# Gating v: the first column piece of six blocks from x times scale, 1/rms and shift row at the read-out

## The chip, the cores and the metric

The kernel runs on one core of a Trainium2 chip. The metric is the device time of one execution, in microseconds (us). Engines are named as in the profile: PE (TensorE, with its weight loads as PEld), DVE (VectorE), ACT (ScalarE), POOL (GpSimd) and SP, which here only issues transfers. SBUF is the on-chip memory, PSUM the banks that PE accumulates into.

## The reference, cut to what matters

A prompt of 1024 rows and a sample of 32 rows, each 1024 wide, go through two layers. The change touches only the start of the first one: the conditioned norm, and the half v of the gating product.

```python
mod = silu(c) @ w_ada[i] + b_ada[i]
sh1, sc1, gt1, sh2, sc2, gt2 = split(mod, 6)
h = rmsnorm(x, g_norm[i, 0]) * (1 + sc1) + sh1
z = gelu(h @ w_in)
u, v = split(z, 2)
v = rmsnorm(v, g_v)
```

Prompt and sample have a conditioning row each. After it come a spatial mix of v in chunks of 128 rows, an output product, and a squared-ReLU channel product. The second layer has a pooling mixer in place of the gating. All is float32; a product of two float32 matrices is made of three products of split operands, high·high, low·high and high·low, where the high part is the operand rounded to the type fp32r and the low part is the rest.

## The kernel before

x is kept transposed in SBUF: three tiles of columns, of 384, 384 and 256 + 32 rows of the input (`acc[t]`). A tile is cut in blocks of 128: 0 to 2, 3 to 5, 6 and 7, and the sample's 32 rows as block 8. Each block is loaded, its squares are summed on ACT (L565), it is turned by eight PE transposes into PSUM (L580) in two halves, and DVE (L586) and ACT (L588) copy these to `acc`.

The conditioning vectors are slices of 256 columns of `mod`: slices 0 to 3 give the shift, 4 to 7 the scale `coef` = (1 + sc1)·g, later ones the rest. Slices 0 to 7 are multiplied on PE (L477), turned on DVE and gathered by small PE products (L459). From slice 8 on they are multiply-adds on DVE (tiles `aa`), two loads of 512 KB for each slice.

The norm of a tile needs 1/rms of its rows as a row spread over partitions. `spread` (L715) takes mean square, square root, reciprocal and one Newton step (DVE and ACT), ACT makes diagonal matrices of the result (L730), PE multiplies them with ones (L732, tile `pb_h`), and ACT copies the product (L893). `apply` (L853) then makes, for each of the eight k blocks of 128 features, mt = x·coef·r on DVE, the high part hh = mt + shift on ACT (L875) and the low part hl on DVE.

v has 2048 columns, worked on in four column pieces p of 512. For each piece the weight comes in four loads q of 256 rows of K (512 KB, through three raw slots). ACT makes its high part wh (L422), DVE its low part wl. A block of a piece is 24 products of 512 columns (8 k blocks × hh·wh, hh·wl, hl·wh), then `v_end` takes it out of PSUM: gelu on ACT (L941), square with a sum on ACT (L942), store.

All loads are in one list, `stream`, in order, issued on SP's queue as soon as their slot is free; `stream_to(kind, key)` steps through it and does what belongs to each item. `issue` (L395) issues, `do_w` splits a weight, `do_ada_pe` and `do_ada` do slices. The order of instructions up to the end of the sixth block is written out by hand (`tc.manual_schedule()`, L991 to L1047): instructions are issued on each engine in the written order.

That order is: x 0 to 2, statistics of tile 0, slices 4 and 0, weight 0, h of tile 0, then products of blocks 0 to 2 with the weight rows of q = 0 (`early_mm`, L973), the same for tile 1 with blocks 3 and 4, and so on for q = 1 to 3, with slices 4 + q and q ahead of each. Blocks 0 to 2 accumulate in the three banks `ps_dn` ("pd"), blocks 3 and 4 in the two banks `ps_up` ("pu"). Then follow the transposes of blocks 6 to 8, block 5 as a whole in a bank of `ps_ms` ("pm", three slots, which transposes, gathers and spreading use too), and the end, `v_end` of blocks 0 to 5 in turn with the weights of column piece 1:

```python
        ps = ps_ms("pv0_5")
        v_mm(ps, 0, 5, range(KB))
        next(h2)
        early_end((0,))
        stream_to("w", ("v", 1, 1))
```

After it comes the loop over `v_order` (L1073 to L1085): piece 1 for blocks 0 to 5, pieces 0 and 1 for blocks 6 to 8, pieces 2 and 3 for all. There a planner, `weave`, puts steps of the load list and other work between the blocks, by an estimate of the time that PE and DVE have used (`time["pe"]`, `time["dve"]`). pv1_0 below means piece 1 of block 0. L79 is the helper that records every DVE arithmetic instruction, so DVE's work is told apart by tile names.

Of the kernel before, what the change touches and what calls it, by code (L numbers as in the profile page):

```python
# [34 lines left out]
def tile_stream_encoder_step(  # L35
# [144 lines left out]
    def load_vectors(i, part):  # L180
        at = sum(k for _, k in rows[i][: part.start])
        for ap, k in rows[i][part]:
            nc.scalar.dma_start(vec_rows[i][at : at + k, :P], ap)
            at += k
# [6 lines left out]
    def turn_conditions():  # L191
        raw = vec_rows[2]
        nc.vector.memset(csil32, 0.0)
        act(out=raw[0:16, P : 2 * P], in_=raw[0:16, :P], func=AF.Silu)

        act(out=raw[0:16, 2 * P : 2 * P + 1], in_=epsT[0:16, :], func=AF.Sqrt)
# [181 lines left out]
    state = {"issued": 0, "next": 0, "raw": 0, "used": 0, "folds": 0}  # L378
    deferred = []

    def in_raw(k):
# [5 lines left out]
    x_rows = [  # L387
        room("h", t, f"x_rows{t}")
        .rearrange("p k n -> p (k n)")[:, : ncol[t] // P * D]
        .rearrange("p (b k n) -> p b k n", k=KB, n=P)  # L390
        for t in range(NT)
    ]
    junk = room("l", NT - 1, "xsq")

    def issue():  # L395
        while state["issued"] < len(stream):
            k = state["issued"]
            kind, key, ap, shape = stream[k]
            if in_raw(k):
                if state["raw"] == RAW_SLOTS:  # L400
                    return
                state["raw"] += 1
                r = t_raw(f"raw{k}")
            elif kind == "x":
                r = x_rows[key // 3][:, key % 3] if key < 8 else junk[:, :, P : 2 * P]
# [12 lines left out]

    def do_w(key, r):
        wh = work.tile([P, 1024], F32R, tag="W", bufs=W_SLOTS, name="wh_" + "_".join(map(str, key)))  # L420
        wl = work.tile([P, 1024], F32R, tag="W", bufs=W_SLOTS, name="wl_" + "_".join(map(str, key)))
        act(out=wh, in_=r, func=AF.Copy)  # L422
# [140 lines left out]
    def x_squares(b, r):  # L563
        nr = P if b < 8 else DEC
        act(  # L565
            out=junk[:nr, :, :P],
            in_=r[:nr],
            func=AF.Square,
            accum_out=ssx[:nr, b : b + 1],
        )  # L570

    def x_turn(b, r):
# [3 lines left out]
        for half in range(2):  # L576
# [8 lines left out]
            if half == 0 or t == 0:  # L585
                nc.vector.tensor_copy(dst, src)  # L586
            else:
                act(out=dst, in_=src, func=AF.Copy)  # L588


    x_turns = deque()

    def do_x(b, r):
        x_squares(b, r)
        if b < 3:
            x_turn(b, r)
        else:
            x_turns.append(lambda: x_turn(b, r))
# [10 lines left out]
    def stream_step():  # L609
# [18 lines left out]
        if in_raw(k):  # L628
            state["raw"] -= 1
# [84 lines left out]

    def spread(t, ss, tag, out, dg):  # L715
# [5 lines left out]
        ts(ms[:, :nb], ss[:, :nb], 1.0 / D, EPS, op0=ALU.mult, op1=ALU.add)  # L721
        act(out=r0[:, :nb], in_=ms[:, :nb], func=AF.Sqrt)
        nc.vector.reciprocal(out=r0[:, :nb], in_=r0[:, :nb])
        tt(out=q[:, :nb], in0=r0[:, :nb], in1=r0[:, :nb], op=ALU.mult)
        stt(out=q[:, :nb], in0=q[:, :nb], scalar=-0.5, in1=ms[:, :nb], op0=ALU.mult, op1=ALU.mult)
        stt(out=r0[:, :nb], in0=q[:, :nb], scalar=1.5, in1=r0[:, :nb], op0=ALU.add, op1=ALU.mult)
        yield False
        pb = ps_ms(f"pb_{tag}")
        for b, (c0, w) in enumerate(blk):
            act(out=dg[:w, c0 : c0 + w], in_=ident[:w, :w], func=AF.Copy, scale=r0[:w, b : b + 1])  # L730
        for b, (c0, w) in enumerate(blk):
            mm(pb[:, c0 : c0 + w], ones[:w, :], dg[:w, c0 : c0 + w], start=True, stop=True)  # L732
        out.append(pb)
# [119 lines left out]
    def apply(t, l, cf, sh, r, keep=False):  # L853
        hh[t] = room("h", t, f"hh{l}_{cf}_{t}", F32R)
        hl[t] = room("l", t, f"hl{l}_{cf}_{t}", F32R)
# [40 lines left out]

    def products(ps, n, terms):
# [8 lines left out]

    ssqv = small.tile([P, 9, 4], F32, name="ssqv")
# [25 lines left out]
    def v_end(ps, p, b):  # L933
# [3 lines left out]
        if b == 8:  # L937
# [21 lines left out]
    h0, h1, h2 = (first_norm(t) for t in range(NT))  # L959

    def early_mm(bs, q):

        wh, wl = witem[("v", 0, q)]
        for second in (False, True):
            for b in bs:
                t, c0 = b // 3, b % 3 * P
                tick(0.46 if second else 0.92)
                for k in range(2):
                    kb = 2 * q + k
                    a_h, a_l = hh[t][:, kb, c0 : c0 + P], hl[t][:, kb, c0 : c0 + P]  # L970
                    w = slice(k * 512, k * 512 + 512)
                    for a in (a_h,) if second else (a_h, a_l):
                        mm(  # L973
                            early_ps[b],
                            a,
                            (wl if second else wh)[:, w],
                            start=kb == 0 and a is a_h and not second,
                            stop=kb == KB - 1 and second,
                        )
# [5 lines left out]
    def conditions(q):  # L985

        stream_to("ada", (0, 4 + q, 1))
        stream_to("ada", (0, q, 1))
        pe_folds.pop(0)()

    with tc.manual_schedule():  # L991
        load_vectors(2, slice(0, 2))
        issue()
        load_vectors(2, slice(2, 4))
        load_vectors(0, slice(0, 1))
        load_vectors(1, slice(0, 1))
        turn_conditions()
        stream_to("x", 1)
        turn_vectors()
        stream_to("x", 2)  # L1000
        next(h0)
        conditions(0)
        statistics(h0)
        stream_to("w", ("v", 0, 0))
        pe_folds.pop(0)()
        for q in range(4):
            next(h0)
            if q == 0:
                late_lo.pop()()
            early_mm((0, 1, 2), q)  # L1010
            if q == 0:
                stream_to("x", 5)
                next(h1)
                x_turns.popleft()()
                x_turns.popleft()()
                next(h1)
                x_turns.popleft()()
                statistics(h1)
            next(h1)
            if q < 3:  # L1020
                conditions(q + 1)
                stream_to("w", ("v", 0, q + 1))
                early_mm((3,), q)
                pe_folds.pop(0)()
                early_mm((4,), q)
                if q == 2:
                    stream_to("x", 6)
            else:
                early_mm((3, 4), q)
        stream_to("x", 8)  # L1030
        while x_turns:
            x_turns.popleft()()
        next(h2)
        ps = ps_ms("pv0_5")
        v_mm(ps, 0, 5, range(KB))
        next(h2)
        early_end((0,))
        stream_to("w", ("v", 1, 1))
        early_end((1, 2))
        stream_to("w", ("v", 1, 2))  # L1040
        early_end((3,))
        stream_to("w", ("v", 1, 3))
        early_end((4,))
        statistics(h2)
        v_end(ps, 0, 5)
# [13 lines left out]
    rv = small.tile([P, 9], F32, name="rv")  # L1059
    rms = small.tile([P, 9, 2], F32, name="rms")  # L1060

# [11 lines left out]
    v_order = [(1, b) for b in range(6)] + [(p, b) for p in range(2) for b in range(6, 9)]  # L1073
# [600 lines left out]
```

## Time and profile before

| | us |
|---|---|
| three runs | 2173.76, 2173.64, 2171.72 |
| their median | 2173.64 |
| the profiled execution, its own time | 2173.74 |
| its span, first to last instruction | 2171.7 |
| mean granted clock of TensorE | 0.996 |

The profile is of one execution. Its page gives each engine's busy time and groups of instructions with their mean duration. The timeline lists instructions by engine: start, duration, engine, line, operation, output from inputs, shapes, count, and in brackets how long the engine stood idle before and what released it. Runs of like instructions that follow one another stand as one row with a count, and the duration is that of the whole row. A matmul's row lasts until its result is out, while the next one starts earlier, so a stretch of products is priced by the distance of their starts. Of the first 80 us, the table by line has these groups of the stage:

| group, first 80 us | count | busy us | mean ns |
|---|---|---|---|
| v products hh·wh, hl·wh, hh·wl (L973) | 40, 40, 40 | 18.8, 18.2, 11.8 | 471, 456, 414 |
| transposes of x (L580) | 64 | 10.8 | 331 |
| slices on PE (L477) | 128 | 9.1 | 427 |
| h: mt, hh, hl of 384 columns | 16 each | 9.1, 9.1, 9.2 | 613, 615, 616 |
| squares of x, 1024 columns (L565) | 8 | 8.4 | 1051 |

### The profile page before, as it was taken

What the parts mean: (1) busy time and instruction counts of PE and PEld (TensorE: products, weight loads), DVE (VectorE), ACT (ScalarE), POOL (GpSimd) and SP (SyncE); (2) the same over time, 40 slices, a digit from 0 to 9 for tenths busy, and PEclk for the clock granted to TensorE, in tenths of its full rate; (3) what the DMA queues carried; (4) which work ended last, traced back from release to release, by engine and by line L of the source; (5) the groups of instructions that cost most, each with busy time, mean ns of one, the idle gap of its engine ahead of it and who ended that gap; (6) DMA issues with size and microseconds to landing.
All of it is one profiled execution on the core that took longest, in us unless ns stands there. A gap on an engine that the chain in (4) does not pass through costs nothing.

```text
span 2171.7 us, 33210 instructions
## 1 busy us (share of the span) xinstructions
PE 2145.5 (99%) x13214; PEld 2078.1 (96%) x13214; DVE 1431.8 (66%) x2499; ACT 971.3 (45%) x1643; POOL 13.3 (1%) x30
## 2 busy tenths in 40 slices
PE   7999999999999999999999999999999999999998
PEld 5778899999999999999999999999999999999997
DVE  5688647566879548496747879869675554523377
ACT  4633422234447552323445566666555542313354
POOL 0000000000000000000000000000000000000001
PEclk9999999999999999999999999999999999999999
DMA  8386534343437454243645466565455552302255
GB/s 300 119 269 193 173 93 139 90 148 109 147 96 233 132 155 143 87 140 110 196 129 161 141 189 182 171 191 158 141 161 158 157 155 68 98 20 78 69 139 125
DMA packets 383262, 312.95 MB, mean 144 GB/s; under 512 B 39458, under 2 KB 346346, under 8 KB 383108
## 3 DMA queue, kind: packets, MB, share of 16 engines
q1 hardware_dynamic: 380452, 308.64, 46.8%
q8 instruction: 103, 1.69, 0.3%
q10 hardware_dynamic: 2144, 1.41, 0.2%
q0 software_dynamic: 512, 0.79, 0.1%
q14 instruction: 51, 0.42, 0.1%
HBM read 278.95 MB, written 31.84 MB: 143 GB/s over the span
## 4 chain that ended last, share of the span: by engine, by line
PE 93%; DVE 3%; DMA 2%; ACT 1%; issue 1%; ACTq 0%; DVEq 0%; SPq 0%
PE pg L902 11%; PE pg L903 11%; PE pg L904 11%; PE pf L902 11%; PE pf L904 11%; PE pf L903 11%; PE po L902 3%; PE po L903 3%; PE po L904 3%; PE pu L902 3%; PE pu L904 3%; PE pu L903 3%; PE pv L929 2%; PE pv L930 2%; PE pv L931 2%; PE pp L1532 1%
## 5 line engine op out<-in xcount | busy, mean ns | idle before, releaser
L902 PE MATMUL pg<-fh,wh_dn 128*128 128x384 f32 (+1 forms) x1536 | 495.8, 323 | 0.0
L902 PE MATMUL pf<-hh,wh_up 128*128 128x384 f32 (+1 forms) x1536 | 494.4, 322 | 0.0
L903 PE MATMUL pf<-hl,wh_up 128*128 128x384 f32 (+1 forms) x1536 | 493.1, 321 | 0.0
L904 PE MATMUL pf<-hh,wl_up 128*128 128x384 f32 (+1 forms) x1536 | 492.9, 321 | 0.2 <-DVE wl_up L79 0.2
L903 PE MATMUL pg<-fl,wh_dn 128*128 128x384 f32 (+1 forms) x1536 | 492.6, 321 | 0.4 <-DVE fl L79 0.4
L904 PE MATMUL pg<-fh,wl_dn 128*128 128x384 f32 (+1 forms) x1536 | 492.5, 321 | 0.0
L79 DVE TENSOR_TENSOR wl_up<-raw,wh_up 128x1024 fp32r<-128x1024 f32 x152 | 185.9, 1224 | 165.4 <-ACT wh_up L422 165.4
L902 PEld LDWEIGHTS pg<-fh,wh_dn 128*128 128x128 f32 x1536 | 288.3, 188 | 1.5 <-ACT fh L1121 0.6
L903 PEld LDWEIGHTS pg<-fl,wh_dn 128*128 128x128 f32 x1536 | 288.3, 188 | 1.5 <-DVE fl L79 0.7
L904 PEld LDWEIGHTS pf<-hh,wl_up 128*128 128x128 f32 x1536 | 288.6, 188 | 0.5 <-DVE wl_up L79 0.5
L903 PEld LDWEIGHTS pf<-hl,wh_up 128*128 128x128 f32 x1536 | 288.3, 188 | 0.4
L902 PEld LDWEIGHTS pf<-hh,wh_up 128*128 128x128 f32 x1536 | 288.2, 188 | 0.4
L904 PEld LDWEIGHTS pg<-fh,wl_dn 128*128 128x128 f32 x1536 | 288.3, 188 | 0.0
L422 ACT ACTIVATE wh_up<-raw 128x1024 fp32r<-128x1024 f32 x152 | 161.2, 1060 | 279.9 <-PE pf L903 213.6
L79 DVE TENSOR_TENSOR acc<-acc,pg 128x384 f32<-128x384 f32 (+1 forms) x336 | 174.2, 519 | 146.3 <-PE pg L904 145.7
L422 ACT ACTIVATE wh_dn<-raw 128x1024 fp32r<-128x1024 f32 x152 | 160.8, 1059 | 202.9 <-PE pg L903 170.6
L79 DVE TENSOR_TENSOR wl_dn<-raw,wh_dn 128x1024 fp32r<-128x1024 f32 x152 | 186.0, 1224 | 82.4 <-ACT wh_dn L422 82.2
L79 DVE SCALAR_TENSOR_TENSOR aa<-raw,csil,aa 128x512 f32<-128x512 f32 (+1 forms) x364 | 203.5, 623 | 8.0 <-DMA raw<-in_w_ada_dram 7.9
L1295 ACT ACTIVATE r<-pf 128x384 f32<-128x384 f32 (+1 forms) x192 | 86.6, 451 | 201.9 <-PE pf L904 199.2
L79 DVE TENSOR_TENSOR fl<-r,fh 128x384 fp32r<-128x384 f32 (+1 forms) x192 | 100.3, 523 | 85.4 <-ACT fh L1121 84.3
L902 PE MATMUL pu<-hh,wh_u 128*128 128x384 f32 (+1 forms) x384 | 125.8, 328 | 0.0
L902 PE MATMUL po<-ush,wh_o 128*128 128x384 f32 (+1 forms) x384 | 123.5, 322 | 0.0
(263 smaller groups left out, 2927.2 us busy)
## 6 DMA issues: line engine op xcount, KB each, us to landing
raw<-in_ffn_w_up_dram SPq DMA_DIRECT2D x152, 512.0 KB, 3.9
raw<-in_ffn_w_down_dram SPq DMA_DIRECT2D x152, 512.0 KB, 3.5
raw<-in_w_ada_dram SPq DMA_DIRECT2D x96, 512.0 KB, 4.3
raw<-in_sgu_w_in_dram SPq DMA_DIRECT2D x40, 512.0 KB, 4.4
xd<-acc SPq DMA_DIRECT2D x8, 1536.0 KB, 7.8
raw<-in_sgu_w_out_dram SPq DMA_DIRECT2D x24, 512.0 KB, 4.0
xo_r<-xd SPq DMA_DIRECT2D x32, 384.0 KB, 3.4
vd<-vt SPq DMA_DIRECT2D x32, 256.0 KB, 4.5
```

Source lines behind the costliest of these rows:

```text
L79: return op(out, *args, **kw)
L422: act(out=wh, in_=r, func=AF.Copy)
L902: mm(ps[:, :n], wh, rh, start=i == 0, stop=False)
L903: mm(ps[:, :n], wh, rl, start=False, stop=False)
L904: mm(ps[:, :n], wl, rh, start=False, stop=i == last)
L929: mm(ps[:m, :], a_h, wh[:, o : o + 512], start=k == 0, stop=False)
L930: mm(ps[:m, :], a_h, wl[:, o : o + 512], start=False, stop=False)
L931: mm(ps[:m, :], a_l, wh[:, o : o + 512], start=False, stop=k == KB - 1)
L1295: act(out=r[:, :n], in_=ps[:, :n], func=AF.Relu)
L1532: mm(ps[:, :n], wg[:, k, e * P : (e + 1) * P], A(t, 2 * g + k), start=k == 0, stop=k == 1)
```

## The change

For blocks 0 to 5 the first column piece of v (p = 0) is no longer multiplied from h but from x·scale: h·W = (x·coef·W)·r + shift·W, where r is 1/rms of the row, a scalar for each partition at the read-out. In parts:

- `scaled` makes the operands from `acc`: hx = x·coef on ACT, lx = x·coef − hx on DVE, in the rooms that hh and hl take later. Neither r nor the shift slices are needed for it.
- `shift_products` multiplies the shift, split in two columns, with the 8 k blocks of wh and wl: 16 products of 512 columns into `prow`, one row copied by ACT. `spread_shift` multiplies it with ones (one float32 product of 512 columns, `pbias`) and ACT copies it to an SBUF tile, `bias`.
- In `v_end`, for p = 0 and blocks 0 to 5, one DVE multiply-add makes ps·r + bias ahead of gelu, which now reads SBUF.
- `roots` makes r from the sums of squares (Abs_reciprocal_sqrt and a Newton step in place of square root, reciprocal and Newton step), per partition into `rv`.
- h itself is still needed for the other pieces. `full` spreads r as before and runs `apply` into the same tiles: for tile 0 between the products of blocks 3 to 5, for tile 1 between the products of pv1_0 and pv1_1.
- Blocks 3, 4 and 5 go together now; block 5 accumulates in its `ps_ms` slot from the start of that group. The transposes of blocks 6 to 8 follow the bias product, and the spreading of tile 1's r, pv1_0, and the spreading of tile 2's r follow them on PE.
- The load list is: x0, slice 4, weight 0, x1, x2, slice 5, weight 1, slice 6, weight 2, x3 to x5, slice 7, weight 3, slices 0 to 3, x6 to x8, then as before. At most eight early loads (slices and x5) are in flight. Low parts of piece 0's weights are made at written places (`late_lo`).
- g_norm, b_ada, pool_scale and g_v are loaded over POOL's queue instead of ACT's, and x2 over SP's instead of ACT's.

The instructions after pv1_2 stand in the same order on each engine as before.

```diff
-    for b in range(3):
-        add_x(b)
     for q in range(4):
-        for j in (8 + 2 * q, 9 + 2 * q, 2 * q, 2 * q + 1):
+        if q == 0:
+            add_x(0)
+        for j in (8 + 2 * q, 9 + 2 * q):
             add_ada(0, j)
         add_w(*v_item(0, q))
-        if q == 0:
-            for b in range(3, 6):
-                add_x(b)
+        for b in ((1, 2), (), (3, 4, 5), ())[q]:
+            add_x(b)
+    for j in range(8):
+        add_ada(0, j)
...
+            if k < first_ada and (kind == "ada" or key == 5):
+                if state["early"] == W_SLOTS // 2:
+                    return
+                state["early"] += 1
...
-                i = (nc.scalar if key == 2 else nc.sync).dma_start(
+                i = nc.sync.dma_start(
...
-        if key == ("v", 0, 0):
-            late_lo.append(lambda: tt(out=wl, in0=r, in1=wh.bitcast(F32), op=ALU.subtract))
+        if key[:2] == ("v", 0):
+
+            def low():
+                tt(out=wl, in0=r, in1=wh.bitcast(F32), op=ALU.subtract)
+                state["raw"] -= 1
+                issue()
+
+            late_lo.append(low)
...
+    def scaled(t, ks, c0, w):
...
+        for k in ks:
+            act(
+                out=hh[t][:, k, c0 : c0 + w],
+                in_=A(t, k, c0, w),
+                func=AF.Copy,
+                scale=coef[:, 0, 0, 0, k : k + 1],
+            )
+        for k in ks:
+            stt(
+                out=hl[t][:, k, c0 : c0 + w],
+                in0=A(t, k, c0, w),
+                scalar=coef[:, 0, 0, 0, k : k + 1],
+                in1=hh[t][:, k, c0 : c0 + w].bitcast(F32),
+                op0=ALU.mult,
+                op1=ALU.subtract,
+            )
+
+    def full(t):
+        cp = t_c(f"r_h0_{t}")
+        pb = diagonals(t, rv[:, 3 * t : 3 * t + 3], [(c * P, P) for c in range(3)], cp, f"h0_{t}")
+        act(out=cp[:, : ncol[t]], in_=pb[:, : ncol[t]], func=AF.Copy)
+        yield False
+        yield from apply(t, 0, 0, 0, cp, keep=True)
...
-        if b == 8:
+        if p == 0 and b < 6:
+            stt(out=vt, in0=ps, scalar=rv[:, b : b + 1], in1=bias[0], op0=ALU.mult, op1=ALU.add)
+            z = vt
+        elif b == 8:
...
+    def shift_products():
...
+        prow = ps_ms("prow")
+        for k in range(KB):
+            for w in witem[("v", 0, k // 2)]:
+                mm(
+                    prow[0:2, :],
+                    parts_of_shift[:, k, :],
+                    w[:, k % 2 * 512 : k % 2 * 512 + 512],
...
+    def spread_shift(row):
+        pbias = ps_ms("pbias")
+        mm(pbias, ones[0:2, :], row[0:2, :], start=True, stop=True)
+        bias.append(work.tile([P, 512], F32, tag="aa", bufs=2, name="shift_rows"))
+        act(out=bias[0], in_=pbias, func=AF.Copy)
...
+    front, rear = (0, 1, 2), (3, 4, 5)
...
+        scaled(0, (6, 7), 0, 3 * P)
+        x_turn(5)
+        x_squares(4)
+        x_squares(5)
+        early_mm(front, (6, 7), False)
+        late_lo.pop()()
+        scaled(1, (0, 1), 0, 3 * P)
+        early_mm(front, (6, 7), True)
+        roots_of(0)
+        slice_(0)
+        early_ps.append(ps_ms("pv0_5"))
+        early_mm(rear, (0, 1), False)
+        fold()
+        f0 = full(0)
+        next(f0)
...
+        early_mm(rear, (6, 7), False)
+        row = shift_products()
+        early_mm(rear, (6, 7), True)
+        spread_shift(row)
+        next(f0)
+        roots_of(1)
+        early_end((0,))
         stream_to("x", 8)
...
+        weights(1, 0)
+        early_end((1,))
+        weights(1, 1)
+        next(f0)
+        early_end((2,))
+        weights(1, 2)
+        for b in (6, 7, 8):
+            x_squares(b)
+            x_turn(b)
+        weights(1, 3)
+        early_end((3, 4, 5))
+        f1 = full(1)
+        next(f1)
+        ps = ps_dn("pv1_0")
+        v_mm(ps, 1, 0, range(KB))
         next(h2)
...
+        next(f1)
+        next(f1)
+        v_end(ps, 1, 0)
+        ps = ps_dn("pv1_1")
+        v_mm(ps, 1, 1, range(KB))
+        next(f1)
+        next(f1)
+        v_end(ps, 1, 1)
         statistics(h2)
+        ps = ps_dn("pv1_2")
+        v_mm(ps, 1, 2, range(KB))
+        v_end(ps, 1, 2)
...
-    v_order = [(1, b) for b in range(6)] + [(p, b) for p in range(2) for b in range(6, 9)]
+    v_order = [(1, b) for b in range(3, 6)] + [(p, b) for p in range(2) for b in range(6, 9)]
```

More of the change, by code (lines that the diff above doesn't have):

```diff
@@ L377, in tile_stream_encoder_step @@
     loads = {}
-    state = {"issued": 0, "next": 0, "raw": 0, "used": 0, "folds": 0}
+    state = {"issued": 0, "next": 0, "raw": 0, "used": 0, "folds": 0, "early": 0}
     deferred = []
@@ L570, in x_squares, with x_turn @@
         )
-    def x_turn(b, r):
+    def x_turn(b):
+        r = x_rows[b]
         t = min(b // 3, 2)
@@ L627, in stream_step @@
         state["next"] += 1
-        if in_raw(k):
+        if k < first_ada and (kind == "ada" or key == 5):
+            state["early"] -= 1
+        if in_raw(k) and not (kind == "w" and key[:2] == ("v", 0)):
             state["raw"] -= 1
@@ L720, in spread @@
         ms, r0, q = t_st(f"ms_{tag}"), t_st(f"r0_{tag}"), t_st(f"q_{tag}")
[L721 to L726, printed above, removed]
-        yield False
[L728 to L733, printed above, removed]
+        roots(r0[:, :nb], ms[:, :nb], q[:, :nb], ss[:, :nb])
+        yield False
+        out.append(diagonals(t, r0, blk, dg, tag))
         yield False
@@ L904, in products @@
             mm(ps[:, :n], wl, rh, start=False, stop=i == last)
+    rv = small.tile([P, 9], F32, name="rv")
+    rms = small.tile([P, 9, 2], F32, name="rms")
+    parts_of_shift = small.tile([P, KB, 2], F32R, name="parts_of_shift")
+    bias = []
     ssqv = small.tile([P, 9, 4], F32, name="ssqv")
@@ L1001, in tile_stream_encoder_step @@
[L1001 to L1029, printed above, removed]
@@ L1030, in tile_stream_encoder_step @@
-        stream_to("x", 8)
-        while x_turns:
-            x_turns.popleft()()
-        next(h2)
[L1034 to L1043, printed above, removed]
+        slice_(4)
+        x_squares(0)
+        fold()
+        weights(0, 0)
+        scaled(0, (0, 1), 0, P)
```

186 lines of the change are left out of this document (136 added, 50 removed).

## The prediction

> **What bounds the kernel now.** I read the page first (span and busy time of each engine), then the waits of PE after 86 us, then the busy time of stretches, then the timelines of PE, ACT and DVE up to 115 us.
>
> ```profile
> span 2171.7 us, 33210 instructions
> PE 2145.5 (99%) x13214; PEld 2078.1 (96%) x13214; DVE 1431.8 (66%) x2499; ACT 971.3 (45%) x1643; POOL 13.3 (1%) x30
> ...
> PE pv L930 <- DVE wl_v L79: 1.6, 1, 1.6
> PE psp L1213 <- DMA vl<-vd: 0.7, 1, 0.7
> ```
>
> PE is busy 99% of the span. The last two rows are all of its waits from 86 to 330 us. So from the second column piece of v on, the end is the moment at which PE gets to a mark, plus a fixed amount of products. Everything that the change touches lies ahead of about 150 us, and behind it PE's instructions stand in the same order in both programs. My sum is therefore the shift of one mark: the first product of column piece 1 for block 0 (pv1_0). Only 26.2 us of the span are without a PE instruction, so a gain is bounded by that; a loss isn't.
>
> ```profile
> 6.79 3.68 PE L580 MATMUL xT<-ident,x_rows 128*128 128x128 f32 x16
> ...
> 10.39 1.18 PE L206 MATMUL rowT<-ident,row 64*128 64x64 f32 x3
> ...
> 13.40 3.45 PE L477 MATMUL ada<-raw,csil 128*32 128x256 f32 x32
> ...
> 19.77 0.79 PE L973 MATMUL pv<-wh_v,hh 128*128 128x512 f32 x1 [1.85 <-ACT hh L875]
> ...
> 45.53 1.93 PE L477 MATMUL ada<-raw,csil 128*32 128x256 f32 x32
> 47.28 0.22 PE L459 MATMUL adat<-adas,squares 128*32 128x4 f32 x8
> ...
> 68.20 2.04 PE L580 MATMUL xT<-ident,x_rows 128*128 128x128 f32 x16
> ...
> 76.60 0.94 PE L732 MATMUL pb_h<-r_h,ones 128*128 128x128 f32 x6
> 77.47 0.51 PE L929 MATMUL pv<-wh_v,hh 128*128 128x512 f32 x1
> ...
> 86.67 0.50 PE L930 MATMUL pv<-wl_v,hh 128*128 128x512 f32 x1 [1.59 <-DVE wl_v L79]
> ...
> 95.43 0.39 PE L929 MATMUL pv<-wh_v,hh 128*128 128x512 f32 x1
> ...
> 112.20 0.39 PE L931 MATMUL pv<-wh_v,hl 128*128 128x512 f32 x1
> ```
>
> The first product of v starts at 19.77, the mark stands at 77.47, and behind it PE loses 1.59 at 86.67. With that loss the mark of before counts as 77.47 + 1.59 = 79.1. From 95.43 to 112.20 lie 74 products, so a product of 512 columns takes 0.227.
>
> **The front, up to the end of the sixth block of piece 0.**
>
> ```profile
> out_dram<-turned POOLq DMA_DIRECT2D x16, 48.0 KB, 3.0
> ...
> row<-in_b_ada_dram ACTq DMA_DIRECT2D x1, 48.0 KB, 4.2
> ...
> row<-in_sgu_g_v_dram ACTq DMA_DIRECT2D x1, 8.0 KB, 5.1
> ```
>
> These are transfers with their queue, size and time to land. Removed from the way to the first product are the statistics of tile 0 and one of two slices of the conditioning. PE starts with 8 transposes (half of 3.68) and the row transposes (1.18), at 6.79, so the first slice starts at 9.8. Before, the way from the first slice (13.40) to the first product (19.77) was 6.4; one slice less takes 1.7 off, the statistics some more. I put the first product at 14. The bounds are 12.7 (the slice and about 1.2 for turning, gathering and scaling) and 17 (the old way of 6.4 from 9.8, plus rows that land late, since g_norm, b_ada and two more now come over POOL's queue; the nearest transfer on that queue takes 3.0 to land, those rows took 4.2 to 5.1 on ACT's, so little lies in the queue itself).
>
> From there PE has in its order, all before the end of the new bias product: 144 products of v (32.7), transposes of blocks 1 to 5 (40 at 2.04/16, 5.1), seven slices (half of 1.93 each, 6.8), seven gathers (half of what two took, about 0.22 each, 1.5), one spreading product (0.94), and, new, 16 products of the shift row (16 × 0.227 = 3.6) and its spreading. This last one is of the kind of pb_h with 512 columns instead of 384: 1.25 by that row, 0.23 if it went like a product of v; I take 1.25. Sum 51.9.
>
> ```profile
> 20.00:80.00 60.00, 56.49 (x358) 41.26 (x359) 32.36 (x67) 30.20 (x58) 0.00 (x0) 0.92 0.54 185
> 34.00:36.00 2.00, 0.31 (x8) 0.00 (x0) 1.84 (x5) 1.82 (x3) 0.00 (x0) 1.00 1.08 386
> 36.00:38.00 2.00, 1.96 (x13) 1.59 (x14) 1.72 (x4) 0.00 (x0) 0.00 (x0) 0.59 1.09 385
> 38.00:40.00 2.00, 2.00 (x13) 1.21 (x12) 0.68 (x3) 0.00 (x0) 0.00 (x0) 0.56 1.09 382
> ```
>
> ```profile
> 40.04 1.14 ACT L875 ACTIVATE hh<-mt,shift 128x384 fp32r<-128x384 f32 x2 [4.22 <-DVE mt L79]
> ```
>
> ```profile
> 40.69 1.15 DVE L79 SCALAR_TENSOR_TENSOR hl<-mt,shift,hh 128x384 fp32r<-128x384 f32 x2 [0.16 <-ACT hh L875]
> ```
>
> In the first view the columns are the stretch, its length, busy time of PE, PEld, DVE, ACT, POOL, then granted clock, DMA share and GB/s. Before, PE was idle for 3.5 of the 60 us, and lost (1 − 0.92) × 60 = 4.8 to the clock. The new front waits in other places (the late low half of wv 0, the scaled copies of k 6 and 7 behind three x squares on ACT). I take 4 for waits (bounds 0 and 8) and 3.4 for the clock (bounds 0 and 6.8). So the bias product ends at 14 + 51.9 + 4 + 3.4 = 73.3, bounds 64 to 84. The other two rows, a pair each of ACT and DVE, price the new scaling: 16 tile-wide instructions per engine of 0.57, 9.1, which lie in this stage, where DVE and ACT have 27 and 30 us free. Before, at 76.60, PE had done the same 144 products and the transposes of blocks 6 to 8 as well: the front brings next to nothing, since the 4.9 of shift products eat what the early start gives.
>
> **The read-out.** Before, block 5 of piece 0 was multiplied alone after the transposes of blocks 6 to 8, and its 5.5 us on PE covered the read-out of the others. Now block 5 is in the rear group. What PE has after the bias product is in this order: transposes of block 6 (8), of 7, of 8, the spreading of tile 1's 1/rms, pv1_0. Each of them hangs on ACT or DVE: three ps_ms slots exist, pv0_5 holds one until it is read out, so the first transposition of block 7 waits for ACT's copy of block 6, and the spreading waits for diagonals that ACT makes only after the read-out of all six blocks. ACT's queue up to that copy begins with the copy of the bias rows, which needs the bias product: nothing of it can be done earlier.
>
> ```profile
> 63.52 1.05 ACT L565 ACTIVATE xsq<-x_rows 128x1024 f32<-128x1024 f32 x1
> ...
> 69.27 0.60 ACT L588 ACTIVATE acc<-xT 128x512 f32<-128x512 f32 x1 [3.44 <-PE xT L580]
> ...
> 71.10 0.20 ACT L722 ACTIVATE r_h<-ms_h 128x3 f32<-128x3 f32 x1
> 72.13 0.91 ACT L730 ACTIVATE r_h<-ident,r_h 128x128 f32<-128x128 f32 x3 [0.84 <-DVE r_h L79]
> 73.06 1.28 ACT L941 ACT_TABLE_LOAD   x1
> ...
> 77.50 0.58 ACT L941 ACTIVATE vt<-pv 128x512 f32<-128x512 f32 x1
> ...
> 78.74 0.58 ACT L941 ACTIVATE vt<-pv 128x512 f32<-128x512 f32 x1
> ...
> 79.98 1.04 ACT L422 ACTIVATE wh_v<-raw 128x1024 fp32r<-128x1024 f32 x1
> ```
>
> ```profile
> 69.71 0.69 DVE L586 COPY acc<-xT 128x512 f32<-128x512 f32 x1 [0.18 <-PE xT L580]
> ...
> 70.85 0.16 DVE L79 TENSOR_SCALAR ms_h<-ssx 128x3 f32<-128x3 f32 x1
> ...
> 81.06 1.23 DVE L79 TENSOR_TENSOR wl_v<-raw,wh_v 128x1024 fp32r<-128x1024 f32 x1 [2.01 <-ACT wh_v L422]
> ...
> 102.71 0.65 DVE L79 SCALAR_TENSOR_TENSOR hl<-mt,shift,hh 128x256 fp32r<-128x256 f32 x2
> 103.80 5.64 DVE L79 SCALAR_TENSOR_TENSOR aa<-raw,csil,aa 128x256 f32<-128x256 f32 x14
> ```
>
> ```profile
> raw<-in_w_ada_dram SPq DMA_DIRECT2D x96, 512.0 KB, 4.3
> ```
>
> ```profile
> DMA to landing us min/median/max: 3.7/5.6/8.8
> ```
>
> ACT's timeline, DVE's, the median landing of a conditioning load, and the landings of the x loads.
>
> gelu and square of a block take 78.74 − 77.50 = 1.24. The new multiply-add out of PSUM is not in the trace; the nearest row is DVE's copy of 512 columns out of PSUM, 0.69, which I take (an SBUF multiply-add of 256 takes 5.64/14 = 0.40, which bounds it from below). The two engines hand the work to and fro. From the end of the bias product: bias copy 0.17 + 0.60, one pair of h copies 1.14, rest of their low halves 0.63, ms and root 0.36, table load 1.28 (DVE's next steps, 1.2, lie beside it), block 0 1.24; then weight 0's high part 1.04, low part 1.23, block 1's multiply-add 0.69, gelu and square 1.24; weight 1's high part 1.04 and low part 1.23. That is 11.9. The 0.17 is the gap from a product's 0.39 to its 0.227.
>
> Now the low part of weight 1 frees the raw slot (three exist) for the load of conditioning slice 8, and DVE has six of its multiply-adds in front of weight 2's low part: 4.3 to land, 6 × 0.40 = 2.4, and 1.23. That frees the slot for the second half of slice 8, of which DVE has five ahead of weight 3's low part: 4.3 + 2.0 + 1.23, then block 3's multiply-add 0.69. Sum 16.2. ACT's own list over the same stretch (h of k 6 and 7, block 2, weight 2: 1.14 + 1.24 + 1.04; squares of blocks 6 to 8, their copies, weight 3: 3 × 1.05 + 0.6 + 0.6 + 0.2 + 1.04) is 9.0 and is done before. Then gelu and square of blocks 3, 4, 5 (3.7), the first diagonal 0.3, and the spreading, 0.94 at full clock, 1.8 at half. With some 25 handovers at 0.03 this is 11.9 + 16.2 + 3.7 + 2.1 + 0.8 = 34.7, of which PE works under 5. The bounds: 21.7 if no ACT item ever waited (0.6 + 1.14 + 0.2 + 1.28 + 2 × 1.24 + 2 × 1.04 = 7.8, then 9.0, 3.7, 0.3, and the spreading 0.9), 44 if both loads took 8.8, as the slowest x load did.
>
> Behind the mark: PE was idle for over 15 us and restarts at a clock of 0.5. Before, 36 to 40 us show what follows a stop of 1.7 us: a clock of 0.56 to 0.59 for one stretch of 3.4 us. I take one such stretch, 1.7 lost (bounds 0 and 3.4). The spreading of tile 2 now stands behind pv1_1 and needs diagonals behind that block's gelu and square on ACT: 0.17 + 1.24 + 0.91 = 2.3 of wait (bounds 0 and 4), and its own 0.94, which lay ahead of the mark before.
>
> The Trainium skill, TensorE: Matmul & The Clock Gate, section on HAM oscillation, says that idle gaps of PE over some 3.4 us throttle it to half rate, and that each burst after such a wait starts cold. By that rule the new stop costs such a start, by a kernel without it the time would be 1.7 less; the rows of 34 to 40 us agree, with a shorter stop.
>
> **The sum.** 73.3 + 34.7 + 1.7 + 2.3 + 0.9 = 112.9 against 79.1: 33.8 later. The profiled execution took 2173.74 (2.0 around its span; the median of the runs shown is 2173.64). So 2173.7 + 33.8 = 2207.5.
>
> **Rivals.**
> - ACT alone (0.14): the loads of slice 8 land so early, or DVE's waits are so short, that only ACT's own list counts: 21.7 to 27 in place of 34.7, hence 2194.5 to 2200. For it: before, ACT ran this list from 73 to 83 nearly without a gap. Against it: then no weight's low part and no multiply-add stood between two gelus.
> - DVE stays behind (0.14): between block 5's read-out and the third tile's h, DVE has 50 conditioning multiply-adds (20), h of tile 1 (16 × 0.57 = 9.1), h of tile 2 (16 pairs of 0.65, 10.4) and 5 of turns: 44.6 from about 104, so 149. PE needs the last of that h 165 products after the mark, at about 150.5. From 2 us of lateness on PE waits, up to some 8: 2210 to 2218.
> - Not slower (0.07): the products of PE overtake the wait, so that the read-out is hidden as before. Then the mark stands at 73.3 + 2.7 (transposes) + 0.9, and with tile 2's spreading at 77.8: 2172.4, and with a front at its low bound of 64, 2163. It decides itself at the first transposition of block 7: if that follows block 6 at once, this is the case. Against it: PE's timeline shows its products only in the order of the program, and before, too, it stood still for a weight (86.67) with later blocks ready.
> - The change doing no early product at all (0.01) would show a first product of v at 19.8 and the read-out's stop all the same, 2213.
>
> **How the numbers follow.** The forecast has 0.64, its own range 2200 to 2216 by the front's likely bounds (68 to 80). With the two slower rivals the range is 2193 to 2220. A difference under 0.2% (4.3 us) is about what can't be told from no change: faster 0.03, same 0.05, slower 0.92.
>
> **What would show it.** Right: PE's first product of v near 14; a wait of PE on ACT of over 12 us at the first transposition of block 7 around 75 to 95 us, another of 5 to 12 at the spreading of tile 1; clock 0.5 there; all later groups of PE with unchanged time; span 30 to 40 longer. Wrong: PE's busy share over 90% between 70 and 110 us, or the bias product ending before 64 or after 84, or new waits of PE after 150 us.

## The result, and the profile after

| kernel | median us | lowest, highest | runs |
|---|---|---|---|
| before | 2172.70 | 2171.72, 2173.76 | 4 |
| changed | 2208.55 | 2206.48, 2210.87 | 4 |

The ratio is 1.0165, with a 95% interval from 1.0148 to 1.0183: the change costs 35.9 us. The profiled execution of the changed kernel took 2208.88, its span is 2207.1.

The page of the changed kernel, first its span and the engines' busy time:

```profile
span 2207.1 us, 33314 instructions
## 1 busy us (share of the span) xinstructions
PE 2153.7 (98%) x13232; PEld 2080.8 (94%) x13232; DVE 1443.5 (65%) x2519; ACT 985.0 (45%) x1669; POOL 15.3 (1%) x34
```

The span grew by 35.4. PE's busy time grew by 8.2, so the time without a PE instruction grew by 27.2, from 26.2 to 53.4. Where it lies is told by PE's waits from the start to 340 us (what PE waited for, us in total, how often, the longest):

```profile
PE xT L603 <- ACT acc L611: 17.4, 1, 17.4
PE pb_h L739 <- DVE sums L553: 8.7, 1, 8.7
...
PE pb_h L739 <- ACT r_h L737: 2.8, 1, 2.8
```

Before, PE had no wait at its transposes, and at the spreading products only one of 1.0 (at 30.09). All three stand behind the bias product, as PE's timeline shows (start, duration, what, and in brackets the idle time ahead and its releaser):

```profile
14.84 0.79 PE L1032 MATMUL pv<-wh_v,hx 128*128 128x512 f32 x1 [0.92 <-ACT hx L928]
...
76.43 1.12 PE L1079 MATMUL pbias<-shift_row,ones 2*128 2x512 f32 x2
77.48 1.41 PE L603 MATMUL xT<-ident,x_rows 128*128 128x128 f32 x8
96.33 2.04 PE L603 MATMUL xT<-ident,x_rows 128*128 128x128 f32 x8 [17.43 <-ACT acc L611]
...
108.45 1.65 PE L739 MATMUL pb_h<-r_h,ones 128*128 128x128 f32 x6 [8.75 <-DVE sums L553]
109.75 0.77 PE L987 MATMUL pv<-wh_v,hx 128*128 128x512 f32 x1
...
125.22 1.11 PE L739 MATMUL pb_h<-r_h,ones 128*128 128x128 f32 x6 [2.77 <-ACT r_h L737]
```

Block 6 is turned at 77.48, block 7 only at 96.33; the spreading of tile 1's 1/rms, which needs ACT's diagonals, starts at 108.45 (the releaser named, a DVE reduction, has nothing to do with it; ACT's diagonals begin at 108.01). The first product of pv1_0 is at 109.75. The stretch from the bias product to there (length, busy time of PE, PEld, DVE, ACT, POOL, granted clock, DMA share, GB/s):

```profile
77.50:111.00 33.50, 6.95 (x34) 5.54 (x34) 24.70 (x51) 21.98 (x43) 0.00 (x0) 0.57 0.40 133
```

In 33.5 us PE works 7. But neither DVE (24.7) nor ACT (22.0) is busy all the time: they wait for each other. ACT's timeline over the first rounds and the last:

```profile
82.79 1.04 ACT L437 ACTIVATE wh_v<-raw 128x1024 fp32r<-128x1024 f32 x1
85.78 0.63 ACT L1002 ACTIVATE vt<-vt 128x512 f32<-128x512 f32 x1 [1.95 <-DVE vt L79]
...
100.10 1.04 ACT L437 ACTIVATE wh_v<-raw 128x1024 fp32r<-128x1024 f32 x1
104.17 0.63 ACT L1002 ACTIVATE vt<-vt 128x512 f32<-128x512 f32 x1 [3.03 <-DVE vt L79]
...
108.01 0.97 ACT L737 ACTIVATE r_h<-ident,rv 128x128 f32<-128x128 f32 x3
```

And DVE's:

```profile
83.86 1.23 DVE L79 TENSOR_TENSOR wl_v<-raw,wh_v 128x1024 fp32r<-128x1024 f32 x1 [2.42 <-ACT wh_v L437]
85.00 0.74 DVE L79 SCALAR_TENSOR_TENSOR vt<-pv,rv,shift_rows 128x512 f32<-128x512 f32 x1
88.14 1.23 DVE L79 TENSOR_TENSOR wl_v<-raw,wh_v 128x1024 fp32r<-128x1024 f32 x1 [2.39 <-ACT wh_v L437]
...
93.26 0.62 DVE L79 TENSOR_SCALAR aa<-raw,csil 128x256 f32<-128x256 f32 x2 [0.87 <-DMA raw<-in_w_ada_dram]
...
102.25 1.22 DVE L79 TENSOR_TENSOR wl_v<-raw,wh_v 128x1024 fp32r<-128x1024 f32 x1
103.39 2.06 DVE L79 SCALAR_TENSOR_TENSOR vt<-pv,rv,shift_rows 128x512 f32<-128x512 f32 x3
```

One round reads: ACT makes the high part of a weight (82.79), DVE waits for it and makes the low part (83.86), and only then takes the next block out of PSUM (85.00); ACT waits for that with its gelu (85.78), and so on. Each engine stands still while the other works. Waits for the loads of slice 8 are there too, but short (0.87 at 93.26, 0.67 at 100.27).

### The profile page after: what moved, and what is told of

It is laid out like the page before. It is cut to its first block, busy times and chain, and to the rows that moved or that the text cites. A ratio compares the mean times of both kernels' runs of the same rounds, so it can differ in the third digit from the quotient of the medians.

```text
span 2207.1 us, 33314 instructions
## 1 busy us (share of the span) xinstructions
PE 2153.7 (98%) x13232; PEld 2080.8 (94%) x13232; DVE 1443.5 (65%) x2519; ACT 985.0 (45%) x1669; POOL 15.3 (1%) x34
## 4 chain that ended last, share of the span: by engine, by line
PE 94%; DVE 2%; DMA 2%; ACT 1%; issue 1%; POOL 0%; DVEq 0%; POOLq 0%
PE pf L956 11%; PE pg L956 11%; PE pf L958 11%; PE pf L957 11%; PE pg L957 11%; PE pg L958 11%; PE pu L956 3%; PE pu L958 3%; PE pu L957 3%; PE po L956 3%; PE po L957 3%; PE po L958 3%; PE pv L987 2%; PE pv L989 2%; PE pv L988 2%; PE pv L1032 2%
## 5 line engine op out<-in xcount | busy, mean ns | idle before, releaser
L958 PE MATMUL po<-ush,wl_o 128*128 128x384 f32 (+1 forms) x384 | 123.1, 321 | 0.0
```

The lines of the kernel that those rows point to most:

```text
L958: mm(ps[:, :n], wl, rh, start=False, stop=i == last)
```

## The experiments

Nine kernels were compared with the kernel before, in three groups. "First pv1_0" and "first product behind v" (the first weight load of the tiles `pu`) are from each kernel's trace; behind the latter all kernels do the same.

| kernel | median us | before, same group | ratio, 95% interval | first pv1_0 | first product behind v |
|---|---|---|---|---|---|
| changed | 2208.55 | 2172.70 | 1.0165 (1.0148 to 1.0183) | 109.75 | 274.9 |
| slice 8 behind the read-out | 2207.61 | 2172.21 | 1.0166 (1.0151 to 1.0181) | 108.78 | 274.3 |
| turns ahead of the bias | 2210.22 | 2172.21 | 1.0176 (1.0161 to 1.0191) | 111.61 | 275.3 |
| no multiply-add | 2203.23 | 2172.21 | 1.0144 (1.0127 to 1.0161) | 103.59 | 269.1 |
| bias ahead of block 5 | 2203.37 | 2172.21 | 1.0143 (1.0128 to 1.0158) | 104.27 | 269.4 |
| multiply-add ahead of low part | 2202.99 | 2170.93 | 1.0145 (1.0131 to 1.0159) | 101.34 | 269.5 |
| no shift row | 2202.68 | 2170.93 | 1.0142 (1.0126 to 1.0157) | 102.14 | 268.6 |
| rows on ACT's queue | 2206.56 | 2172.66 | 1.0159 (1.0145 to 1.0172) | 106.60 | 273.2 |
| shift slices ahead | 2172.00 | 2170.93 | 1.0004 (0.9995 to 1.0013) | 76.67 | 237.7 |
| the same, three edits more | 2168.13 | 2172.66 | 0.9981 (0.9972 to 0.9990) | 73.53 | 234.4 |

In the trace of the kernel before the first product behind v is at 237.6. Against the kernel before of its own group, the changed kernel costs 35.9 us and the nine cost 35.4, 38.0, 31.0, 31.2, 32.1, 31.8, 33.9, 1.1 and −4.5, in the order of the table; the intervals reach 2 to 4 us to either side. So a difference of one or two us between kernels is told by the traces alone, one execution of each, whose starts differ too: in the changed kernel and the six that load and start as it does, the first product of v lies between 14.37 and 15.18.

**Do the loads of slice 8 set the read-out?** Their multiply-adds were queued behind block 5's read-out on DVE:

```diff
+            elif key[:2] == (0, 8):
+                with tc.issue_after(state["read"]):
+                    do_ada(*key, r, 256)
```

> Only edit: the multiply-adds of conditioning slice 8 stand behind block 5's read-out on DVE. If the two loads of slice 8 are what the read-out waits for (the prediction's chain of 16.2 us), two landings of some 3.7 us and eleven multiply-adds of 0.40 leave the chain and ACT's list is next: about 5 us faster than the changed kernel, 2202 to 2205. If ACT's list with its hand-overs to DVE is nearly as long (in the profile after, ACT ends the high part of weight 3 at 101.1, and the multiply-adds of blocks 3 to 5 could follow at about 102.3 in place of 103.4), it is 1 us: 2206 to 2209, with the spreading of tile 1 at 107 to 108 us.

PE's timeline of it has the spreading of tile 1 at

```profile
107.47 1.65 PE L742 MATMUL pb_h<-r_h,ones 128*128 128x128 f32 x6 [7.68 <-ACT r_h L740]
```

1.0 earlier, and no more. Its DVE timeline shows what takes the place of the loads:

```profile
94.97 1.23 DVE L79 TENSOR_TENSOR wl_v<-raw,wh_v 128x1024 fp32r<-128x1024 f32 x1 [2.39 <-ACT wh_v L437]
...
101.27 1.23 DVE L79 TENSOR_TENSOR wl_v<-raw,wh_v 128x1024 fp32r<-128x1024 f32 x1 [1.91 <-ACT wh_v L437]
```

DVE now waits for ACT's high parts (2.39, 1.91). So the loads were on the chain by 1 us only.

**Is it the PSUM slots?** The transposes and squares of blocks 6 to 8 were put ahead of the shift products:

```diff
         fold()
+        stream_to("x", 8)
+        for b in (6, 7, 8):
+            x_turn(b)
         next(f0)
         early_mm(rear, (6, 7), False)
+        for b in (6, 7, 8):
+            x_squares(b)
         row = shift_products()
```

> Only edit: the transposes and squares of blocks 6 to 8 stand ahead of the shift products. If the scarce PSUM slots make the stop (17.4 us at the first transposition of block 7), that stop goes and the time falls to 2188 to 2195. If the order of ACT's and DVE's queues behind the bias product makes it, PE only stands still at the next place, the spreading of tile 1, for over 20 us in one piece, and the time stays within 4 us of the changed kernel, 2205 to 2212 (some 5 us leave the chain, 3 to 8 are put ahead of the bias product).

PE's timeline:

```profile
84.31 1.12 PE L1079 MATMUL pbias<-shift_row,ones 2*128 2x512 f32 x2
110.31 1.65 PE L739 MATMUL pb_h<-r_h,ones 128*128 128x128 f32 x6 [24.88 <-ACT r_h L737]
```

The stop at the transposes is gone, and PE stands still for 24.9 us in one piece at the next place. The bias product is 7.9 later than at 76.43, the chain behind it 6.0 shorter (26.0 between the two starts in place of 32.0), and the time does not fall. It is not the slots.

**Is it the new multiply-add?** It was left out (gelu reads PSUM):

```diff
-        if p == 0 and b < 6:
-            stt(out=vt, in0=ps, scalar=rv[:, b : b + 1], in1=bias[0], op0=ALU.mult, op1=ALU.add)
-            z = vt
-        elif b == 8:
+        if b == 8:
```

> Leaves out the multiply-add at the read-out of blocks 0 to 5 (1/rms and shift row are computed but not used): gelu reads PSUM as before the change. If the new hand-over from DVE to ACT makes the stop, the stop shrinks to what it was before and the time falls by 20 us or more, below 2190. If the place of the whole read-out behind the bias product makes it, only the bias copy (0.6) and the multiply-adds that lie on the chain (four of 0.74, with their hand-overs some 6 in all) are saved: 2201 to 2204.

```profile
92.00 1.12 PE L603 MATMUL xT<-ident,x_rows 128*128 128x128 f32 x4 [13.81 <-ACT acc L611]
...
102.29 1.65 PE L739 MATMUL pb_h<-r_h,ones 128*128 128x128 f32 x6 [5.49 <-DVE aa L79]
```

That is PE's timeline again. Both stops shrink, by 3.6 and 3.3, and 19.3 us of them stay without any multiply-add. pv1_0 starts 6.2 earlier, of which 0.7 lie ahead of the read-out (the bias product is at 75.73 in place of 76.43). So the multiply-add's price is some 5.5 us; the place of the read-out is the rest.

**Does the read-out hang on the bias product alone?** Block 5's 24 products were put behind it:

```diff
-    front, rear = (0, 1, 2), (3, 4, 5)
+    front, rear = (0, 1, 2), (3, 4)
...
         spread_shift(row)
+        early_ps.append(ps_ms("pv0_5"))
+        for ks in ((0, 1), (2, 3), (4, 5), (6, 7)):
+            early_mm((5,), ks, False)
+            early_mm((5,), ks, True)
```

> Only edit: shift products and bias product stand ahead of block 5's 24 products, which are made alone behind them (the products are the same). If the read-out starts with the bias product and has nothing to hide it, PE's 5.4 us of block 5 now lie beside it: 4 to 5.5 us faster than the changed kernel, 2203 to 2205. If the stop ends at a time that loads or earlier work of ACT set, nothing changes: 2207 to 2210.

```profile
90.93 1.98 PE L603 MATMUL xT<-ident,x_rows 128*128 128x128 f32 x8 [12.21 <-ACT acc L611]
...
102.97 1.65 PE L739 MATMUL pb_h<-r_h,ones 128*128 128x128 f32 x6 [8.72 <-DVE sums L553]
```

The first stop shrinks by 5.2 (17.4 to 12.2), which is what 24 products take (24 × 0.227 = 5.4), the second stays at 8.7. Here the products that were put beside the read-out came off the stop nearly whole.

**Is it the order of low part and multiply-add on DVE?** Only that order was turned round:

```diff
         early_end((1,))
+        late_lo.pop(0)()
         weights(1, 1)
         next(f0)
         early_end((2,))
+        late_lo.pop(0)()
...
```

> Only edit: on DVE each low part of a piece-1 weight stands behind the next block's multiply-add instead of ahead of it. If the hand-overs between ACT and DVE (multiply-add, gelu, high part, low part, next multiply-add) make the length of the read-out, ACT's three waits for a multiply-add (6.3 us in the profile after) go: 5 to 8 us faster than the changed kernel, 2200 to 2204, with the spreading of tile 1 at about 101 us. If slice 8's loads or ACT's own list hold it, nothing is gained: 2206 to 2210.

ACT's waits between 75 and 112 us in the changed kernel hold this line:

```profile
ACT vt L1002 <- DVE vt L79: 6.3, 3, 3.0
```

In this kernel they hold this one:

```profile
ACT vt L1002 <- DVE vt L79: 1.6, 2, 1.4
```

And PE's timeline gives

```profile
100.04 1.65 PE L739 MATMUL pb_h<-r_h,ones 128*128 128x128 f32 x6 [5.94 <-ACT r_h L737]
...
118.60 1.78 PE L739 MATMUL pb_h<-r_h,ones 128*128 128x128 f32 x6 [4.73 <-ACT r_h L737]
```

4.7 of ACT's 6.3 went, DVE's waits for ACT's high parts in the same stretch fell from 4.8 to 1.8, and pv1_0 starts 8.4 earlier. 3.0 of that are given back behind it, 2.0 of them ahead of tile 2's spreading, where the wait grew from 2.8 to 4.7, and the first product behind v is 5.4 earlier. By the runs against their own group it is 3.8 us, less than the 5 to 8 expected, and the intervals don't tell 3.8 from 5.4.

**What do the shift products cost?** They were left out, with the bias product:

```diff
-        row = shift_products()
         early_mm(rear, (6, 7), True)
-        spread_shift(row)
+        bias.append(work.tile([P, 512], F32, tag="aa", bufs=2, name="shift_rows"))
+        nc.vector.memset(bias[0], 0.0)
```

> Leaves out the 16 shift products, the bias product and the two copies (the shift row is taken as zero). If all of PE's work ahead of the read-out passes through to the end, their 4.9 us on PE and the bias copy of 0.6 come off: 5 to 7 us faster than the changed kernel, 2201 to 2204. If the start of the read-out hangs on something else (roots of the rear blocks, ACT's h copies), 0 to 2 us: 2206 to 2209.

PE's timeline:

```profile
71.53 1.03 PE L603 MATMUL xT<-ident,x_rows 128*128 128x128 f32 x8
...
102.14 0.77 PE L987 MATMUL pv<-wh_v,hx 128*128 128x512 f32 x1
```

pv1_0 is 7.6 earlier, the first product behind v 6.3. The transposes of block 6, which follow PE's work ahead of the read-out, are 5.9 earlier (71.53 in place of 77.48). The products that were left out took 4.8 of that, this trace's first product is 0.5 earlier (14.37), and 0.6 more lie in the front behind it, where the two kernels do the same. From there to pv1_0 it is 1.7 less, with no bias copy (0.6) on the way. PE's work ahead of the read-out passes through whole. By the runs against their own group it is 4.1 us, with the 5 to 7 expected inside the intervals.

**And the rows on POOL's queue?** They were loaded over ACT's queue again:

```diff
-        load_vectors(nc.gpsimd, 0, slice(0, 1))
-        load_vectors(nc.gpsimd, 1, slice(0, 1))
-        load_vectors(nc.gpsimd, 2, slice(2, 4))
+        load_vectors(nc.scalar, 2, slice(2, 4))
+        load_vectors(nc.scalar, 0, slice(0, 1))
+        load_vectors(nc.scalar, 1, slice(0, 1))
```

> Only edit to the changed kernel: g_norm, b_ada, pool_scale and g_v come over ACT's queue again. They landed after 5.2 to 7.4 us on POOL's queue in the profile after, and PE waited 2.2 us for them. If the start of PE's chain sets the bias product, 1 to 2 us of it arrive there and at the end: 2206 to 2208, first product of v at 13 to 13.5 us. If the loads of weights and x (DMA busy above 1.0 from 15 to 40 us) set the front, the first product is earlier but the bias product is not: 2208 to 2210.

The DMA issues of the changed kernel (the last number is us to landing):

```profile
row<-in_b_ada_dram POOLq DMA_DIRECT2D x1, 48.0 KB, 7.4
```

Those of this one:

```profile
row<-in_b_ada_dram ACTq DMA_DIRECT2D x1, 48.0 KB, 4.5
```

PE's timeline of this one:

```profile
12.53 0.80 PE L1032 MATMUL pv<-wh_v,hx 128*128 128x512 f32 x1 [0.92 <-ACT hx L928]
...
73.38 1.12 PE L1079 MATMUL pbias<-shift_row,ones 2*128 2x512 f32 x2
```

The first product is 2.3 earlier and the bias product 3.1, both more than expected; 1.7 are left at the first product behind v. The time, 2206.56, is in the range expected if PE's start passes through, but the intervals of this kernel and the changed one overlap.

**The read-out beside products.** The version with the shift slices ahead leaves nothing out and changes the order. Its core, with the low parts of piece 1 behind the multiply-adds as above:

```diff
         scaled(0, (6, 7), 0, 3 * P)
         x_turn(5)
+        slice_(0)
...
         early_mm(rear, (2, 3), False)
+        copy_row = shift_products()
...
+        early_mm(rear, (2, 3), True)
+        spread_shift(row)
+        f1 = full(1)
+        next(f1)
+        stream_to("x", 8)
+        early_mm(rear, (4, 5), False)
+        early_end((0,))
+        next(f0)
+        weights(1, 0)
+        early_mm(rear, (4, 5), True)
+        early_end((1,))
+        late_lo.pop(0)()
+        weights(1, 1)
+        early_end((2,))
```

> Nothing left out. The four shift slices, whose loads had landed by about 41 us, are multiplied during the front's last products, shift row and bias product stand between the rear's products, h of tile 0 and the read-outs of blocks 0 to 2 lie beside the rear's products, and low parts stand behind the next multiply-add. If the loss is only that the read-out had no products of PE beside it, nearly all of it goes: 33 to 40 us faster than the changed kernel, 2168 to 2176, and PE stands still for no more than 2 us at a time after 45 us. If the algebra itself costs (DVE falls behind with the multiply-adds and the second rounding of x times scale, or PE's clock does), at least 10 us stay: 2182 or more.

It takes 2172.00, 1.0004 of the kernel before, which can't be told from no change. PE's waits from 20 to 150 us are these, all of them:

```profile
PE pv L1032 <- DVE wl_v L79: 1.1, 1, 1.1
PE pb_h L739 <- ACT r_h L737: 1.0, 1, 1.0
PE pv L1032 <- DVE lx L79: 0.2, 1, 0.2
```

Busy time in stretches:

```profile
20.00:80.00 60.00, 57.62 (x389) 38.43 (x388) 36.41 (x73) 36.98 (x70) 0.00 (x0) 1.00 0.57 200
80.00:110.00 30.00, 30.00 (x143) 24.73 (x142) 29.30 (x70) 23.63 (x51) 0.00 (x0) 1.00 0.54 173
```

The same stretch of the changed kernel:

```profile
20.00:80.00 60.00, 55.38 (x366) 35.59 (x364) 27.37 (x59) 24.91 (x48) 0.00 (x0) 0.97 0.49 176
```

DVE and ACT do 9 and 12 us more up to 80, beside products that PE has anyway, and behind it PE doesn't stop: block 7's transposes, which the written order now puts between the products of pv1_0, follow without a wait.

```profile
79.71 1.04 PE L603 MATMUL xT<-ident,x_rows 128*128 128x128 f32 x8
```

The last version aims at the waits that were left: rows over ACT's queue, the low part of weight 0 ahead of the copies of blocks 1 and 2, the spreading of tile 1 behind the rear's (4, 5) products. The last two, as edits of the version with the shift slices ahead:

```diff
         early_mm((0,), (0, 1), False)
+        late_lo.pop()()
         stream_to("x", 2)
         x_turn(1)
         x_turn(2)
-        late_lo.pop()()
...
         spread_shift(row)
-        f1 = full(1)
-        next(f1)
...
         early_mm(rear, (4, 5), True)
+        f1 = full(1)
+        next(f1)
         early_end((1,))
```

> The version with the shift slices ahead, and three edits: rows on ACT's queue, the low part of weight 0 ahead of the copies of blocks 1 and 2, and the spreading of tile 1's 1/rms behind the (4, 5) products of the rear. They aim at the waits left in that version (2.2 + 1.0 for rows, 1.1 for the low part, 1.0 at the spreading). If PE's own work sets this version from 15 us on, 2 to 4 us come off: 2167 to 2170, below the kernel before. If DMA sets the front up to 40 us, under 1 us: 2171 to 2172.

2168.13, ratio 0.9981 with an interval from 0.9972 to 0.9990: 0.19% below the kernel before, and the interval stays clear of no change by 0.1%. Its first product is at 13.02 in place of 15.29, its first pv1_0 at 73.53. The waits for the rows' landing and for the low part are gone; the one at the spreading of tile 1 is not (0.8 in place of 1.0).

## Why the prediction held, point by point

The forecast was 2207.5 by a mark that moves from 79.1 to 112.9. Its steps against the trace:

- **First product**, 14 forecast: 14.84, inside 12.7 to 17. Not right was that little lay in POOL's queue itself: the rows landed after up to 7.4 there, and with ACT's queue the first product came 2.3 earlier in both pairs of kernels that differ in the queue.
- **Bias product's end**, 73.3 forecast, bounds 64 to 84: 77.5. 0.8 of the 4.2 is the first product. Waits came to 3.4 (1.1, 2.2 and 0.2 in PE's timeline), 4 forecast; the clock to about 3.6 (the first four products and 16 transposes at half rate, 0.8 and 1.6, six products at 46 us, 1.2), 3.4 forecast. The mis-sized term is the product: 0.227 was measured in long rows of them, while here, in PE's timeline of the changed kernel,

```profile
56.85 0.50 PE L1032 MATMUL pv<-wh_v,hx 128*128 128x512 f32 x1
...
59.81 0.24 PE L480 MATMUL adat<-adas,squares 128*32 128x4 f32 x8
59.98 1.66 PE L1032 MATMUL pv<-wl_v,hx 128*128 128x512 f32 x6
61.57 1.07 PE L498 MATMUL ada<-raw,csil 128*32 128x256 f32 x16
```

  12 products lie between 56.85 and 59.81 and six between 59.98 and 61.57, 0.25 and 0.265 each: some 4 us over 144, with the gathers between them.
- **Read-out**, 34.7 forecast: 77.5 to the first product of pv1_0, 32.3. Up to the end of the low part of weight 1 it was 11.9, as forecast; from there to the end of block 3's multiply-add 14.7, 16.2 forecast. The chain over the two loads of slice 8 was there as described, but it was the longest by a hair only: without it the read-out is 1 us shorter. The step that was wrong is that ACT's list "is 9.0 and is done before" with room to spare, over 5 us by the forecast's terms. ACT's work was 8.7, but ACT stood still for 3.0 within it (0.6 and 1.35 for DVE, 1.1 for a transposition), so its high part of weight 3 ended at 101.1, 11.8 behind the low part of weight 1, and DVE's low part of weight 3 began 1.1 later. Loads and hand-overs were nearly tied.
- **Behind the mark**, one stretch at half clock (1.7), a wait of 2.3 and 0.9 forecast: eight products up to 0.43 apart (1.7), a wait of 2.77, and 1.0. A second stretch at half clock behind that wait (1.5) was not forecast. By the rule of the Trainium skill (TensorE: Matmul & The Clock Gate, HAM oscillation), that a gap over some 3.4 us brings a cold start, the first one follows; the second came after a gap of 2.8, which that rule doesn't give. The shorter stop before, 1.7 us, is not covered by it either.
- **Sum**: the first product behind v is 37.3 later, 33.8 forecast; 1.9 comes back up to the end, the cause of which stays open, and the span is 35.4 longer. That 33.8 came so close is in part luck: the front was put 4.2 too short and the read-out 2.4 too long, and the second stretch at half clock was left out.

The signs that it named for being right were there: a stop of 17.4 at the first transposition of block 7, one of 8.75 at the spreading of tile 1, a granted clock of 0.50 from 108 to 113, a span 35.4 longer, and no new wait of PE of over 1 us behind 150.

Of the rivals, "ACT alone" had the right engine and too short a list: the hand-overs it left out made it nearly as long as the forecast's chain. "DVE stays behind" didn't come: behind 130 us PE has no wait for h, though DVE is 98% busy from 110 to 130. "Not slower" is the time that the version with the shift slices ahead reaches, but by its written order, not by PE overtaking a wait; in the changed kernel block 7 did not follow block 6 at once, which by the prediction's own point of decision speaks against this rival.

The experiments show the cause. At the first product behind v the multiply-add is worth 5.8 us, the shift row 6.3 and the order of the low parts 5.4 (0.4 to 1.1 of each lies in the start and front of that trace), and all of the loss goes when the same work, with nothing left out, lies beside products. That last version also has the better order of the low parts and moves other work of ACT and DVE forward, so what the products alone give isn't separated in it; it is in the experiment on block 5, 5.2 us of stop for 5.4 of products. Open is whether the kernel before could gain 4 us too by putting its own waits elsewhere; that was not tried.

## What to carry to other kernels

A read-out moved to DVE, or put behind a late operand (here the shift row), needs products of the matmul engine that don't depend on it; count the us of such products and compare them with the chain of hand-overs, not with the busy time of either engine. Where two engines feed each other in turn, the order of two instructions on one of them can be worth as much as an operation that is left out. A stop that moves to the next instruction when its own place is freed shows that the queue behind it, not the place, is the limit.

## What the runs showed of the hardware that had not been expected

At the start PE ran at half rate while the clock column of the windows shows full speed. Of the changed kernel, a window and PE's timeline:

```profile
10.00:20.00 10.00, 7.89 (x46) 5.60 (x46) 3.07 (x9) 2.35 (x4) 0.00 (x0) 1.00 1.07 397
```

```profile
15.43 0.63 PE L1032 MATMUL pv<-wh_v,lx 128*128 128x512 f32 x1
15.85 0.63 PE L1032 MATMUL pv<-wh_v,hx 128*128 128x512 f32 x1
...
16.71 3.62 PE L603 MATMUL xT<-ident,x_rows 128*128 128x128 f32 x16
```

Products stand 0.42 apart, and 16 transposes take 3.62, where 2.04 were shown before. Later the column does show the half rate. A pause of 2.2 us ahead of 43.06 was followed by a clock of 0.50 from 45 to 48, and one of 2.8 (ahead of 125.22) by eight products up to 0.43 apart:

```profile
125.00:130.00 5.00, 4.78 (x16) 3.81 (x17) 4.81 (x14) 1.08 (x4) 0.00 (x0) 0.68 0.64 195
```

That the pauses brought it is not shown by a run that changes them alone; the pauses of up to 1.1 in the version with the shift slices ahead left the clock at 1.00 from 20 to 110.
